# The first layer's input: norm gains applied behind the transposition, quarters of x prepared between the products

## The chip, the cores and the metric

The kernel runs on one core of a Trainium2 chip. The metric is the device time of one execution in microseconds; lower is better. The core has TensorE (PE in the profile, its weight loads PEld), VectorE (DVE), ScalarE (ACT), GpSimd (POOL), the SyncE queue that issues the transfers (SP), and 16 DMA engines.

## The reference

Two transformer-like blocks follow one another on x of 256 tokens by 1024 channels, in float32. What the change touches is the entrance of the first layer of the first block:

```
h = rmsnorm(x, norm1_g[l])          # x * rsqrt(mean(x*x) + eps) * g
z = h @ w_in[l]                     # w_in[l]: 1024 x 6616
z_mla, z_nsa, z_fox, z_dsa, z_gate = split_cols(z, ...)
```

Four mixers work on the columns of z (latent attention, MLA, takes the first 416), gates mix them, w_out and a feed-forward layer follow, all of it twice, and then the second block. The division by the root mean square is by token, the gain g by channel.

## The kernel before

The 256 tokens are two tiles t = 0, 1 of 128. A product needs its left side transposed (channels on the partitions), in chunks k of 128 channels: xT holds 8 chunks for both tiles. Every float32 matrix is split into a rounded part and a rest (h or "hi", and lo), and each product of a chunk is three matmuls: hi by hi (L189), hi by lo (L190), lo by hi (L195). For an xT of 8 chunks and one block of columns, a tile takes 24 matmuls, in two groups of 12 (`products`, L184).

Weights come through `unit` (L60): four chunks by up to 512 columns, as two transfers into `raw` (two chunks each, 504 KB here), then for each half a cast to `whi` on ACT (L85) and a subtraction to `wlo` on DVE (L88). `raw` has six buffers. `steps` (L108) runs, for one block of columns, over k0 = 0 and 4: one unit, then the group of t = 0 and the group of t = 1, so the first block of 504 columns of w_in is four groups of 12 products: (k0 0, t 0), (0, 1), (4, 0), (4, 1). In this text they are steps 1 to 4. `zc(0)` is that block.

x is prepared in quarters (t, c), c a half of the channels. `prep_half` (L392) multiplies a quarter by the gain on DVE (`xg`, L396); `split_T` transposes four chunks on PE into a PSUM tile `tp` (L218), one ACT cast makes xTh (L236) and one DVE subtraction xTl (L237). `square` (L402) takes sums of squares by token on ACT, and `rms_stats` (L407) makes of them on POOL the factor by which the products are scaled when they leave PSUM (L533, L535).

`block1` (L428) writes the order at the start by hand: x(0,0) and the first half of the gain, broadcast to 128 partitions, are loaded; quarter (0,0) is prepared; then the first unit is loaded, with x(0,1) and the second half of the gain between its two transfers; quarter (0,1); then both quarters of t = 1, and the squares. `spin` (L267) puts 12 matmuls on constants ahead of all this on PE.

The framework is a planner: it schedules every engine's instructions in an order of its own, by priority (the order of the program) among what its cost model holds ready, and draws the waits. `issue_after(ins)` keeps what is traced under it behind `ins` on the engine of `ins`, and says nothing to other engines. An engine runs its queue in that order, whatever is late.

After `zc(0)` come `rope_tables` (28 small memsets, a chain of small DVE operations, two sines on ACT, copies on POOL), constants on POOL, and MLA interleaved with the next blocks of columns; MLA normalises its part of z with a POOL power (`rsq`, L257) and transposes the result on PE.

Of the kernel before, what the change touches and what calls it, by code (L numbers as in the profile page):

```python
# [9 lines left out]
F32 = mybir.dt.float32  # L10
# [4 lines left out]
AF = mybir.ActivationFunctionType  # L15
ALU = mybir.AluOpType
AX = mybir.AxisListType

P = 128
T = 256  # L20
D = 1024
# [18 lines left out]
class Net:  # L40
# [16 lines left out]

    def unit(self, w, k0, nk, c0, cn, after=None):  # L60
        nc = self.nc
        if self.ready is not None:
            r, self.ready = self.ready, None
            return r
        src = w.rearrange("(k p) n -> p k n", p=P)
        raws = []
        for i in range(0, nk, 2):
            m = min(2, nk - i)
            raw = self.raw_half()
            nc.sync.dma_start(raw[:, :m, :cn], src[:, k0 + i:k0 + i + m, c0:c0 + cn])  # L70
            raws.append(raw)
            if i == 0 and after is not None:
                after()
        hs, ls = [], []
        for k in range(0, nk, 2):
            for _ in range(min(self.bg_rate // 2, len(self.bg))):
                self.bg.pop(0)()
            m, raw = min(2, nk - k), raws[k // 2]
            self.count += 1
            wp, sfx, nb = self.wp, "", 5  # L80
            if self.wp2 and self.count % 7 in (3, 6):
                wp, sfx, nb = self.wp2, "2", 2
            h = wp.tile([P, 2, 512], F32R, name="whi" + sfx, bufs=nb)
            lo = wp.tile([P, 2, 512], F32R, name="wlo" + sfx, bufs=nb)
            nc.scalar.copy(h[:, :m, :cn], raw[:, :m, :cn])  # L85
            self.turn += 1
            eng = nc.gpsimd if self.share and self.share[self.turn % len(self.share)] else nc.vector
            eng.tensor_sub(lo[:, :m, :cn], raw[:, :m, :cn], h[:, :m, :cn].bitcast(F32))  # L88
# [95 lines left out]
    def products(self, o, xT, k0, t, hs, ls, first, last, within=None):  # L184
        nc, n = self.nc, len(hs)
        later, self.later = self.later, []
        for k in range(n):
            sh, sl = self.chunk(xT, k0 + k, t)
            nc.tensor.matmul(o, sh, hs[k], start=first and k == 0, stop=False)  # L189
            nc.tensor.matmul(o, sh, ls[k], start=False, stop=False)  # L190
            if k == 2 and within is not None:
                within()
            if k % 2 == 1 or k == n - 1:
                for j in range(k - k % 2, k + 1):
                    nc.tensor.matmul(o, self.chunk(xT, k0 + j, t)[1], hs[j], start=False, stop=last and j == n - 1)  # L195
        for f in later:
            f()
# [78 lines left out]

    def constants(self):
        nc, c = self.nc, self.const
        self.spin(12)
        self.ident = c.tile([P, P], F32, name="ident")  # L280
        ones = c.tile([P, 2, P], F32, name="ones")
        nc.vector.memset(ones, 1.0)
# [106 lines left out]

    def prep_half(self, t, c, g, xT, ssq, square=True):  # L392
        nc = self.nc
        sl = slice(c * 512, (c + 1) * 512)
        xg = self.act.tile([P, 512], F32, name="xg", bufs=2)
        nc.vector.tensor_mul(xg, self.x[t][:, sl], g[:, sl])  # L396
        last = self.split_T(xg, 4, xT, c * 4, t)
        if square:
            self.square(t, c, ssq)
        return last  # L400

    def square(self, t, c, ssq):  # L402
        junk = self.act.tile([P, 512], BF16, name="junk", bufs=1)
# [3 lines left out]
    def rms_stats(self, ssq, what):  # L407
# [11 lines left out]
            return r, h  # L419
        return r, None  # L420

    def new_xT(self):
        return self.pair(self.act, 8, "xT")

# [3 lines left out]
    def block1(self):  # L428
        nc, a = self.nc, self.a
        xT, ssq = self.new_xT(), self.new_ssq()  # L430
        x = a["x"]
        g = self.act.tile([P, D], F32, name="gain", bufs=1)
        src = a["norm1_g"][0]

        def load(t, c):
            sl = slice(c * 512, (c + 1) * 512)
            nc.sync.dma_start(self.x[t][:, sl], x[0, t * P:(t + 1) * P, sl])

        def load_gain(c):
            nc.sync.dma_start(g[:, c * 512:(c + 1) * 512],  # L440
                              bass.AP(tensor=src.tensor, offset=src.offset + c * 512, ap=[[0, P], [1, 512]]))

        def second():
            load(0, 1)
            load_gain(1)

        load(0, 0)
        load_gain(0)
        last = self.prep_half(0, 0, g, xT, ssq[0], square=False)
        with self.tc.issue_after(last[0].ins), self.tc.issue_after(last[1].ins):  # L450
            self.ready = self.unit(a["w_in"][0], 0, 4, 0, 504, after=second)
            last = self.prep_half(0, 1, g, xT, ssq[0], square=False)
        with self.tc.issue_after(last[0].ins), self.tc.issue_after(last[1].ins):
            for c in range(2):
                load(1, c)
            for c in range(2):
                self.prep_half(1, c, g, xT, ssq[1])
            for c in range(2):
                self.square(0, c, ssq[0])
        with self.tc.tile_pool(name="b1const", bufs=1) as cpool:  # L460
            self.cpool = cpool
            for l in range(DEPTH):
                r = [self.rms_stats(ssq[t], "half") for t in range(2)]
                xT, ssq = self.attn_layer(l, xT, r)
                r2 = [self.rms_stats(ssq[t], "square")[1] for t in range(2)]
                if l < DEPTH - 1:
                    xT, ssq = self.ff_layer(l, xT, r2)
        self.mp = self.ctx.enter_context(self.tc.tile_pool(name="mem", bufs=1))
        self.block2_constants(self.mp)
        self.memory()  # L470
        return self.ff_layer(DEPTH - 1, xT, r2)[1]
# [48 lines left out]
                self.linear(hT, D_FF // P, a["w_down"][l], [(0, 512), (512, 512)], ev_down)  # L520
        return nxT, ssq

    def attn_layer(self, l, xT, r):
        nc, a = self.nc, self.a
        w = a["w_in"][l]
        with self.tc.tile_pool(name=f"attn{l}", bufs=1) as pool:
# [11 lines left out]
            zc = lambda i: self.steps(xT, 8, w, [(i * 504, 504)], ev_z)  # L538
# [32 lines left out]
            def run(*fill):  # L571
                for f in fill:
                    yield from f

            for _ in zc(0):
                pass
            if l == 0:
                self.rope_tables(self.cpool)
                self.block1_constants(self.cpool)
            self.interleave(self.mla(l, z, oT[0]), run(zc(1), zc(2), zc(3)))  # L580
            self.flush_later()
            self.interleave(self.nsa(l, z, oT[1]), run(zc(4), gates(0), gates(1)))
# [8 lines left out]
            nxT, ssq = self.new_xT(), self.new_ssq()  # L591
# [879 lines left out]
```

## Time and profile before

| | us |
|---|---|
| median of 3 runs | 1733.2 (1732.5 to 1733.45) |
| profiled execution, its own time | 1731.31 |
| its span | 1729.6 |
| PE busy | 1685.1 (97%) |
| DVE busy | 1140.7 (66%) |
| ACT busy | 859.0 (50%) |
| POOL busy | 253.9 (15%) |
| DMA read from HBM | 287.58 MB |

Busy shares are averages over the whole span; the change touches the first 30 us or so of it. The time is the profiled execution's span and 1.7 us around it. PE's clock has two levels, 1.2 and 2.4 GHz; the profile gives the granted share, 0.50 and 1.00.

### The profile page before, as it was taken

To read this page: it belongs to the slowest core of one execution; us is meant where nothing else is said; L and a number is where in the kernel's file an instruction comes from. 1 tells how busy PE (TensorE), PEld (TensorE's weight loads), DVE (VectorE), ACT (ScalarE), POOL (GpSimd) and SP (SyncE) were. 2 spreads that over 40 slices of the span, in tenths; PEclk is the share of its full clock that TensorE was granted. 3 is DMA by queue.
4 is the path that set the end of the run, shared out by engine and by line. 5 is a ranking of instruction groups with operands and counts; after the bars stand their busy time and mean duration, and the time that the engine had idled before them with its cause. 6 is when DMAs were issued, how large, how long until landed. Compare 5 with 4: busy or idle time off the path is not lost. (4 is left out here: it accounts for less than half of the span.)

```text
span 1729.6 us, 22754 instructions
## 1 busy us (share of the span) xinstructions
PE 1685.1 (97%) x8388; PEld 1371.0 (79%) x8388; DVE 1140.7 (66%) x1783; ACT 859.0 (50%) x1300; POOL 253.9 (15%) x283
## 2 busy tenths in 40 slices
PE   8999899999999999999999999999999999999998
PEld 5787678888778767788887977878888977878887
DVE  5766866655466596766456879675555887776554
ACT  5655455554455545555345645444443554544441
POOL 3210100000121011100006830000002850000001
PEclk9999999999999999999999999999999999999999
DMA  7554436555664543665556635366465644456471
GB/s 249 146 146 146 130 120 201 174 183 180 198 167 138 149 124 121 203 196 180 186 181 189 215 127 176 114 196 187 151 220 178 207 145 140 151 191 177 144 226 54
DMA packets 160887, 290.12 MB, mean 168 GB/s; under 512 B 18150, under 2 KB 42056, under 8 KB 160776
## 3 DMA queue, kind: packets, MB, share of 16 engines
q1 hardware_dynamic: 160776, 288.67, 54.5%
q8 instruction: 66, 1.08, 0.3%
q14 instruction: 45, 0.37, 0.1%
HBM read 287.58 MB, written 1.05 MB: 167 GB/s over the span
## 5 line engine op out<-in xcount | busy, mean ns | idle before, releaser
L88 DVE TENSOR_TENSOR wlo<-raw,whi 128x1024 fp32r<-128x1024 f32 (+3 forms) x472 | 571.1, 1214 | 345.1 <-ACT whi L85 338.5
L85 ACT CAST whi<-raw 128x1024 fp32r<-128x1024 f32 (+4 forms) x536 | 546.2, 1022 | 437.3 <-PE mm L195 336.4
L189 PE MATMUL mm<-whi,xTh 128*128 128x512 f32 (+3 forms) x1344 | 522.0, 389 | 3.6 <-DVE th L562 2.1
L190 PE MATMUL mm<-wlo,xTh 128*128 128x512 f32 (+3 forms) x1344 | 512.8, 383 | 0.3 <-DVE wlo L88 0.3
L195 PE MATMUL mm<-whi,xTl 128*128 128x512 f32 (+3 forms) x1344 | 405.4, 382 | 2.2 <-DVE xTl L237 2.0
L189 PEld LDWEIGHTS mm<-whi,xTh 128*128 128x128 f32 x1344 | 253.2, 188 | 49.8 <-DVE th L562 3.0
L195 PEld LDWEIGHTS mm<-whi,xTl 128*128 128x128 f32 x1344 | 249.1, 188 | 51.4 <-DVE xTl L237 4.6
L190 PEld LDWEIGHTS mm<-wlo,xTh 128*128 128x128 f32 x1344 | 253.4, 189 | 42.9 <-DVE wlo L88 1.0
L88 POOL TENSOR_TENSOR wlo<-raw,whi 128x776 fp32r<-128x776 f32 (+1 forms) x64 | 136.7, 2158 | 41.2 <-ACT whi L85 35.9
L257 POOL TENSOR_TENSOR rsq<-rse,mhalf 128x1 f32<-128x1 f32 (+2 forms) x32 | 27.4, 858 | 600.8 <-DVE rse L255 600.8
L189 PE MATMUL mm<-whi,hTh 128*128 128x512 f32 x192 | 76.1, 396 | 0.0
L190 PE MATMUL mm<-wlo,hTh 128*128 128x512 f32 x192 | 75.7, 394 | 0.0
L195 PE MATMUL mm<-whi,hTl 128*128 128x512 f32 x192 | 60.2, 394 | 0.0
L1194 DVE SCALAR_TENSOR_TENSOR mm<-uT,convwT,mm 128x256 f32<-128x256 f32 x120 | 57.8, 481 | 0.1
L1194 DVE SCALAR_TENSOR_TENSOR O<-uT,convwT,O 128x256 f32<-128x256 f32 x120 | 57.8, 481 | 0.0
L189 PE MATMUL mm<-whi,oTh 128*128 128x512 f32 (+1 forms) x140 | 56.6, 404 | 0.0
L190 PE MATMUL mm<-wlo,oTh 128*128 128x512 f32 (+1 forms) x140 | 55.6, 397 | 0.0
L189 PE MATMUL mm<-whi,memTh 128*128 128x512 f32 x128 | 52.7, 412 | 0.0
L190 PE MATMUL mm<-wlo,memTh 128*128 128x512 f32 x128 | 51.0, 399 | 0.0
L410 POOL TENSOR_TENSOR ms<-ssq 128x1 f32<-128x1 f32 x8 | 1.9, 249 | 309.4 <-ACT junk L404 309.3
L236 ACT CAST xTh<-tp 128x512 fp32r<-128x512 f32 x48 | 28.0, 585 | 39.0 <-PE tp L218 37.3
L613 ACT ACTIVATE pexp<-S,nmax 128x128 f32<-128x128 f32 (+1 forms) x80 | 32.6, 419 | 28.6 <-DVE nmax L609 28.4
(404 smaller groups left out, 2367.1 us busy)
## 6 DMA issues: line engine op xcount, KB each, us to landing
raw<-in_w_in SPq DMA_DIRECT2D x80, 512.0 KB, 3.7
raw<-in_w_ffn_in SPq DMA_DIRECT2D x80, 512.0 KB, 4.5
raw<-in_w_up SPq DMA_DIRECT2D x64, 512.0 KB, 3.7
raw<-in_w_down SPq DMA_DIRECT2D x64, 512.0 KB, 4.1
raw<-in_w_ffn_out SPq DMA_DIRECT2D x44, 512.0 KB, 4.2
raw<-in_w_in SPq DMA_DIRECT2D x40, 504.0 KB, 4.2
raw<-in_w_xkv SPq DMA_DIRECT2D x32, 512.0 KB, 4.3
raw<-in_w_in SPq DMA_DIRECT2D x32, 388.0 KB, 3.7
```

The source lines that it names most:

```text
L85: nc.scalar.copy(h[:, :m, :cn], raw[:, :m, :cn])
L88: eng.tensor_sub(lo[:, :m, :cn], raw[:, :m, :cn], h[:, :m, :cn].bitcast(F32))
L189: nc.tensor.matmul(o, sh, hs[k], start=first and k == 0, stop=False)
L190: nc.tensor.matmul(o, sh, ls[k], start=False, stop=False)
L195: nc.tensor.matmul(o, self.chunk(xT, k0 + j, t)[1], hs[j], start=False, stop=last and j == n - 1)
L236: a = nc.scalar.copy(h, tp)
L257: nc.gpsimd.tensor_tensor(r, e, self.mhalf[:, :n], op=ALU.pow)
L410: nc.gpsimd.tensor_tensor(s, ssq[:, 0:1], ssq[:, 1:2], op=ALU.add)
L613: nc.scalar.activation(pe[:, h, :nk], S[h % 2][:, h // 2, :nk], AF.Exp, bias=nm[:, h:h + 1], accum_out=sums[:, h:h + 1])
L1194: nc.vector.scalar_tensor_tensor(o, u, cwT[:, g, j:j + 1], o, op0=ALU.mult, op1=ALU.add)
```

## The change

- The first norm's gain is no longer broadcast over 128 partitions (two transfers of 256 KB). Its row of 1024 is loaded once as 8 by 128 (4 KB), transposed on PE to gT (128 by 8, one column for a chunk), and applied behind the transposition of x: for each chunk an ACT activation with gT as the scale makes the hi part and a DVE operation (times gT, minus hi) the lo part. The DVE multiplication to `xg` goes. For a quarter that is four ACT and four DVE operations of 128x128 instead of one and two of 128x512.
- The spin is 7 matmuls instead of 12. Two matmuls of the identity by quarter (0,0) are added behind that quarter.
- Only quarter (0,0) is prepared ahead of `zc(0)`. Quarters (1,0), (0,1) and (1,1) are loaded and prepared by a hook behind steps 1, 2 and 3. Their ACT and DVE work stands behind that of the quarter before; their PE transposes stand behind the fourth product of the step just traced (`self.second`). The next step is traced behind the new quarter on ACT and DVE, the weights' casts of step 3 among it.
- The squares and `rms_stats` of tile 0 follow quarter (0,1), those of tile 1 quarter (1,1). `rope_tables` and the constants are traced behind the last quarter's ACT and DVE work.
- Later layers keep `prep_half` with a broadcast gain.

```diff
-    def unit(self, w, k0, nk, c0, cn, after=None):
...
+    def unit(self, w, k0, nk, c0, cn):
...
-            if i == 0 and after is not None:
-                after()
...
-            nc.tensor.matmul(o, sh, ls[k], start=False, stop=False)
+            m = nc.tensor.matmul(o, sh, ls[k], start=False, stop=False)
+            if k == 1:
+                self.second = m
...
-        self.spin(12)
+        self.spin(7)
...
+    def order_after(self, ops):
+        s = ExitStack()
+        for o in ops:
+            s.enter_context(self.tc.issue_after(o.ins))
+        return s
...
+        g8 = self.act.tile([P, 512], F32, name="xg", bufs=2)[0:8, :P]
+        gT = self.const.tile([P, 8], F32, name="gainT")
...
-        def second():
-            load(0, 1)
-            load_gain(1)
-
+        def prep(t, c):
+
+            tp = self.transposes([self.x[t][:, c * 512 + k * P:c * 512 + (k + 1) * P] for k in range(4)])
+            for k in range(4):
+                i = c * 4 + k
+                h, lo = self.chunk(xT, i, t)
+                last = (nc.scalar.activation(h, tp[:, k], AF.Copy, scale=gT[:, i:i + 1]),
+                        nc.vector.scalar_tensor_tensor(lo, tp[:, k], gT[:, i:i + 1], h.bitcast(F32),
+                                                       op0=ALU.mult, op1=ALU.subtract))
+            return last
+
+        def arrive(i):
+
+            if i < 3:
+                c, t = (i + 1) // 2, (i + 1) % 2
+                load(t, c)
+                with self.order_after(self.arrived), self.order_after([self.second]):
+                    self.arrived = prep(t, c)
+                if c == 1:
+                    with self.order_after(self.arrived):
+                        for h in range(2):
+                            self.square(t, h, ssq[t])
+                        r.append(self.rms_stats(ssq[t], "half"))
+
+        nc.sync.dma_start(g8, a["norm1_g"][0].rearrange("(k p) -> k p", p=P))
         load(0, 0)
-        load_gain(0)
-        last = self.prep_half(0, 0, g, xT, ssq[0], square=False)
-        with self.tc.issue_after(last[0].ins), self.tc.issue_after(last[1].ins):
-            self.ready = self.unit(a["w_in"][0], 0, 4, 0, 504, after=second)
-            last = self.prep_half(0, 1, g, xT, ssq[0], square=False)
-        with self.tc.issue_after(last[0].ins), self.tc.issue_after(last[1].ins):
-            for c in range(2):
-                load(1, c)
-            for c in range(2):
-                self.prep_half(1, c, g, xT, ssq[1])
-            for c in range(2):
-                self.square(0, c, ssq[0])
+        tg = self.ptp.tile([P, 4, P], F32, name="tp")
+        nc.tensor.transpose(tg[:, 0, :8], g8, self.ident[0:8, 0:8])
+        nc.vector.tensor_copy(gT, tg[:, 0, :8])
+        self.arrived = prep(0, 0)
+        junk = self.pO.tile([P, 4, P], F32, name="O")
+        for _ in range(2):
+            nc.tensor.matmul(junk, self.ident_r, xT[0][:, 0:4, :P], start=True, stop=True)
...
-            for _ in zc(0):
+            first = zc(0)
+            for i in range(4):
+                with self.order_after(self.arrived if hook is not None else ()):
+                    next(first)
+                if hook is not None:
+                    hook(i)
+            for _ in first:
                 pass
             if l == 0:
-                self.rope_tables(self.cpool)
-                self.block1_constants(self.cpool)
+                with self.order_after(self.arrived):
+                    self.rope_tables(self.cpool)
+                    self.block1_constants(self.cpool)
```

## Rows read from the trace of the kernel before

**Rows 1.** Stretches: us, busy (instructions) by engine, granted clock, DMA share, GB/s

```profile
6.60:9.60 3.00, 1.36 (x7) 0.88 (x7) 1.23 (x6) 1.52 (x2) 0.00 (x0) 1.00 0.89 339
9.60:11.70 2.10, 1.11 (x4) 0.72 (x4) 1.81 (x2) 0.56 (x1) 0.00 (x0) 0.51 1.05 408
11.70:16.80 5.10, 4.94 (x12) 3.46 (x11) 2.61 (x4) 3.42 (x6) 0.00 (x0) 0.53 1.07 365
...
18.80:26.80 8.00, 8.00 (x35) 6.31 (x34) 6.77 (x17) 6.65 (x13) 5.27 (x7) 1.00 0.83 259
...
40.00:1729.60 1689.60, 1653.00 (x8266) 1348.89 (x8264) 1116.41 (x1706) 836.71 (x1259) 237.93 (x232) 1.00 0.54 166
```

**Rows 2.** Timeline of DVE to 21 us: start, duration, operation, [idle before and releaser]

```profile
6.02 0.69 DVE L396 TENSOR_TENSOR xg<-x,gain 128x512 f32<-128x512 f32 x1 [3.63 <-DMA gain<-in_norm_g]
...
9.85 0.69 DVE L396 TENSOR_TENSOR xg<-x,gain 128x512 f32<-128x512 f32 x1 [1.01 <-DMA gain<-in_norm_g]
10.46 1.20 DVE L88 TENSOR_TENSOR wlo<-raw,whi 128x1008 fp32r<-128x1008 f32 x1
```

**Rows 3.** Timeline of ACT to 21 us

```profile
8.00 1.03 ACT L85 CAST whi<-raw 128x1008 fp32r<-128x1008 f32 x1
...
16.81 0.63 ACT L404 ACTIVATE junk<-x 128x512 bf16<-128x512 f32 x1
...
17.56 0.63 ACT L404 ACTIVATE junk<-x 128x512 bf16<-128x512 f32 x1
```

**Rows 4.** Timeline of PE, to 17 us and at the end of the first block

```profile
1.53 5.07 PE L275 MATMUL O<-junk 128*128 128x512 bf16 x12 [1.53 <-DVE junk L272]
...
9.09 0.50 PE L189 MATMUL mm<-whi,xTh 128*128 128x504 f32 x1 [1.37 <-ACT whi L85]
10.59 1.12 PE L218 MATMUL tp<-ident,xg 128*128 128x128 f32 x4 [1.00 <-DVE xg L396]
11.71 0.79 PE L190 MATMUL mm<-wlo,xTh 128*128 128x504 f32 x1
...
26.18 0.62 PE L195 MATMUL mm<-whi,xTl 128*128 128x504 f32 x2
```

**Rows 5.** Transfers: SP's issues, landing times (last number, us), DMA rate of two stretches

```profile
0.81 0.39 SPq L437 DMA_DIRECT2D x<-in_x  x1
1.25 0.42 SPq L440 DMA_DIRECT2D gain<-in_norm_g  x1
1.72 0.43 SPq L70 DMA_DIRECT2D raw<-in_w_in  x1
...
x<-in_x SPq DMA_DIRECT2D x1, 256.0 KB, 3.1
...
fox_b<-in_fox_f_bias SPq DMA_DIRECT2D x1, 2.0 KB, 3.1
...
2.80:4.80 2.00, 2.00 (x6) 0.72 (x5) 0.00 (x0) 0.00 (x0) 1.91 (x10) 1.00 0.94 135
5.20:7.20 2.00, 1.73 (x7) 0.67 (x6) 1.12 (x5) 0.00 (x0) 1.04 (x2) 1.00 1.01 380
```

**Rows 6.** Groups of operations by line and shape: busy us, mean ns of one

```profile
L236 ACT CAST oTh<-tp 128x128 fp32r<-128x128 f32 x4 | 1.1, 271 | 0.0
...
L237 DVE TENSOR_TENSOR oTl<-tp,oTh 128x128 fp32r<-128x128 f32 x4 | 1.1, 281 | 0.0
```

**Rows 7.** Timelines of POOL and PE behind the first block, around MLA's normalisation

```profile
31.47 0.88 POOL L374 COPY cos<-cs 128x32 f32<-128x32 f32 x6
...
33.62 0.73 POOL L257 TENSOR_TENSOR rsq<-rse,mhalf 128x2 f32<-128x2 f32 x1
...
35.01 0.56 PE L218 MATMUL tp<-ident,z 128*128 128x128 f32 x3 [2.67 <-DVE z L709]
```

More of the change, by code (lines that the diff above doesn't have):

```diff
@@ L56, in __init__ @@
         self.x = [self.act.tile([P, D], F32, name=f"x{t}") for t in range(2)]
-    def unit(self, w, k0, nk, c0, cn, after=None):
+    def unit(self, w, k0, nk, c0, cn):
         nc = self.nc
-        if self.ready is not None:
-            r, self.ready = self.ready, None
-            return r
         src = w.rearrange("(k p) n -> p k n", p=P)
@@ L388, in apply_rope, with prep_half @@
         eng.tensor_tensor(view[:, :, :rot], view[:, :, :rot], u, op=ALU.add)
-    def prep_half(self, t, c, g, xT, ssq, square=True):
+    def prep_half(self, t, c, g, xT, ssq):
         nc = self.nc
@@ L396, in prep_half @@
         nc.vector.tensor_mul(xg, self.x[t][:, sl], g[:, sl])
[L397 to L400, printed above, removed]
+        self.split_T(xg, 4, xT, c * 4, t)
+        self.square(t, c, ssq)
     def square(self, t, c, ssq):
@@ L430, in block1 @@
         xT, ssq = self.new_xT(), self.new_ssq()
-        x = a["x"]
-        g = self.act.tile([P, D], F32, name="gain", bufs=1)
-        src = a["norm1_g"][0]
+        g8 = self.act.tile([P, 512], F32, name="xg", bufs=2)[0:8, :P]
+        gT = self.const.tile([P, 8], F32, name="gainT")
+        r = []
         def load(t, c):
             sl = slice(c * 512, (c + 1) * 512)
[L437 to L441, printed above, removed]
@@ L443, in second @@
-        def second():
-            load(0, 1)
-            load_gain(1)
-        load(0, 0)
-        load_gain(0)
-        last = self.prep_half(0, 0, g, xT, ssq[0], square=False)
-        with self.tc.issue_after(last[0].ins), self.tc.issue_after(last[1].ins):
-            self.ready = self.unit(a["w_in"][0], 0, 4, 0, 504, after=second)
-            last = self.prep_half(0, 1, g, xT, ssq[0], square=False)
-        with self.tc.issue_after(last[0].ins), self.tc.issue_after(last[1].ins):
-            for c in range(2):
-                load(1, c)
-            for c in range(2):
-                self.prep_half(1, c, g, xT, ssq[1])
-            for c in range(2):
-                self.square(0, c, ssq[0])
+            nc.sync.dma_start(self.x[t][:, sl], a["x"][0, t * P:(t + 1) * P, sl])
@@ L462, in block1 @@
             for l in range(DEPTH):
-                r = [self.rms_stats(ssq[t], "half") for t in range(2)]
-                xT, ssq = self.attn_layer(l, xT, r)
+                if l > 0:
+                    r = [self.rms_stats(ssq[t], "half") for t in range(2)]
+                xT, ssq = self.attn_layer(l, xT, r, arrive if l == 0 else None)
                 r2 = [self.rms_stats(ssq[t], "square")[1] for t in range(2)]
@@ L521, in ff_layer, with attn_layer @@
         return nxT, ssq
-    def attn_layer(self, l, xT, r):
+    def attn_layer(self, l, xT, r, hook=None):
         nc, a = self.nc, self.a
```

## The prediction, made before the changed kernel was run

> **What bounds the kernel now.** I read the busy time by stretches first, then the timelines of PE, DVE and ACT over the first 36 us, then the transfers. From 40 us to the end PE is busy 1653.0 of 1689.6 us at full clock [rows 1]: that part is PE's own work, and whatever PE gains before it should be carried to the end. The change works in the first block of columns, which ends at 26.80 (26.18 and 0.62) [rows 4]. Its 48 products would take 11.0 us at the pace of 18.8 to 26.8, 8.00 us for 35, or 0.229 us each [rows 1]. The reader is to see where the rest goes.
>
> Up to 6.02 DVE waits for a gain, not for x: 3.63 us of idle time end with the transfer of `gain` [rows 2]. While the first broadcast runs, 2.8 to 4.8, the DMA moves 135 GB/s at 94% busy, against 380 GB/s at 5.2 to 7.2 [rows 5]. The second half of the gain does more harm: DVE runs in order, and the multiplication of quarter (0,1) stands ahead of the first wlo. It waits for its gain until 9.85, so wlo runs at 10.46 although its whi was ready at 9.03 (8.00 and 1.03) [rows 2, 3]. PE did its first product at 9.09 and got to the second at 11.71 [rows 4]. In that gap the clock fell: the granted share is 1.00 from 6.6 to 9.6, where PE was busy 1.36 of 3.0 us, and 0.51 to 0.53 from 9.6 to 16.8. There 12 instructions took 4.94 us, 0.41 each [rows 1].
>
> **Term 1, the first products.** The spin's pace is 5.07/12 = 0.42 us, so 7 end at 4.5 instead of 6.6 [rows 4]. x(0,0) takes the second place in SP's queue, issued at about 1.25, and lands 3.1 later as the first transfer did: 4.35 [rows 5]. The gain's 4 KB goes first, at 0.81; no transfer of that kind is in the trace, and the nearest is one of 2 KB that took 3.1: 3.9, hidden under the spin [rows 5]. Five transposes follow, 0.28 us each if at half clock (1.12 for four) [rows 4]: 4.5 to 5.9. The ACT operations of 128x128 take 0.27 each and run behind the transposes one by one [rows 6], so the last ends near 6.2, and whi takes 6.2 to 7.2 [rows 3]; the copy of gT on DVE lies under the transposes, the four DVE operations (0.28 each) under whi. Nothing of a gain stands ahead of wlo now: 7.25 to 8.45, at 1.20 [rows 2]. The second product starts at 8.5 instead of 11.71: **3.2 us earlier**. The two added matmuls wait for the hi part and fit before whi; they cost nothing unless whi were earlier.
>
> Bounds: with transposes at full clock it is 3.9. The other end is the weights. The two transfers ahead of and in raw are 760 KB, 2.0 us at 380 GB/s from the start near 1.6, and the first x shows about 1 us between its last byte and its landing: raw lands near 5. The row says only that it had landed by 8.00, where ACT took it up [rows 3]; if it were still that late, the second product comes at 10.3, and the term is 1.4.
>
> **Term 2, from there to the end of the block.** Before it takes 15.1 us (11.71 to 26.80) [rows 4]. After: 47 products at 0.229, 10.8; three quarters of four transposes at half of 1.12, 1.7; 0.2 for the last matmul to end; and idle time. Step 1 doesn't wait: wlo of the second half is there at 9.65, when PE is still at transposes. Step 2 ends too early for step 3. Its weights' cast stands on ACT behind quarter (0,1), whose transposes stand behind the fourth product of step 2. From the end of these transposes: 0.35 for ACT's last chunks, perhaps a square (0.75, the distance of two squares [rows 3]), whi 1.03, wlo 1.25. That is 3.4 us with a square, 2.6 without; PE has 8 products and the first of step 3 to cover it, 2.1. Idle 0.5 to 1.3; I take 1.3, as the squares are traced earlier than the cast. Quarter (1,1) is covered by the 8 products behind its transposes (1.8, against 0.35 on ACT and 0.3 on DVE). Sum 14.0: **1.1 us shorter**, if the clock stays at 1.00. The gain in DVE work (one 128x512 multiplication of 0.69 for each quarter [rows 2]) is not counted, since DVE isn't last in any of this.
>
> **Term 3, behind the block.** Two squares of tile 1 and four ACT operations for each quarter crowd into the last 4 us, beside the evacuation of tile 0 and the next casts; the 28 memsets and the rope chain now start behind the last quarter. No row shows that order; ACT was busy 6.65 of 8.00 us from 18.8 to 26.8 [rows 1], so 0 to 0.8 is lost: 0.5. SP's loads of positions and of MLA's gains move behind x(1,1), which costs nothing, as they are needed some 10 us later. The wait of 2.67 us at 35.01, where MLA's rsq ran at 33.62, behind six cos copies from 31.47 and what follows them on POOL [rows 7], I leave as long as it is. No added wait stands in SP's queue.
>
> Sum: 3.2 + 1.1 - 0.5 = 3.8 us. The events are those of the profiled execution (1731.31, span 1729.6), which is 1.9 below the median of the runs; taken from the median, 1733.2 - 3.8 = 1729.4.
>
> **The rivals.**
> *The clock falls all the same.* PE's stretch from 6.6 to 9.6 was busy 1.36 of 3.0 us, and the clock fell [rows 1]; after, it holds the added matmuls, one product and 1.1 us from 8.5 on, some 2 us, hardly double. For it: 5 spin matmuls are gone. Against: the idle time of 1.37 us ahead of the first product [rows 4] shrinks to two of under 1 us. If 10 products run at 0.41, 1.8 us go: 1731.3. The Trainium skill ("TensorE: Matmul & The Clock Gate", Part 4: PE-mode transpose) says that transposes don't count as activity for the clock; this speaks against the change, which puts transposes in the place of spin matmuls, and by it this rival would be the likelier one. The trace neither bears it out nor denies it: transposes from 10.59 to 11.71 ran at the low clock, and it rose only when products had run on to 16.8 [rows 1, 4].
> *The weights come no earlier.* Then term 1 is 1.4, the sum 2.0 and the time 1731.2 at full clock. For it: SP's queue held no transfer that landed sooner than 3.1 after its issue, and raw's own landing isn't seen. Against: the 2 us that the gain took are gone from ahead of it [rows 5]. The same time results if 1.8 of the gain go into the wait at 35.01 [rows 7].
> *More than forecast.* With the rms factors done earlier and the rope tables behind MLA's rsq on POOL, the wait of 2.67 goes too [rows 7]: 1726.7.
> *Slower.* The idle time between steps 2 and 3 is the place: if it is as long as that ahead of the second product before (9.6 to 10.6 idle and transposes to 11.7 [rows 4]), as it would be with both squares ahead of the cast, the clock falls a second time. Steps 3 and 4 are 24 products at 0.41, 4.3 us lost, and 10 more in the next block, 1.8; with the first fall (1.8) and term 3 doubled (0.5) the 3.8 become -4.6: 1737.8. [...]
>
> **How the numbers follow.** Forecast 0.43, clock 0.20, weights 0.09, more 0.17, slower 0.11. A measurement of this kernel can tell about 0.2%, 3.5 us, from no change. The forecast's own range is 1728 to 1731 (idle 0.5 to 1.3, term 3 from 0 to 0.8, term 1 to 3.9), and 0.3 of its 0.43 lies over 3.5 us of gain; with the 0.17 and 0.03 of the clock case that is 0.50 for faster. Slower is 0.11, the rest 0.39. The range goes from 1726.2, under the better case, to 1733.4, over the weights' case; it leaves out the slower one and a little of the better.
>
> **What would show it.** Right: the first transposes near 4.6, no wait for a gain on DVE, the second product near 8.5, granted clock 1.00 through 9.6 to 16.8, one idle time of about 1 us ahead of step 3's L190, the block's end near 22.6, and from there the same stretches as before, shifted. Wrong: ACT's first whi waiting for raw; a clock of 0.50 behind 9.6; an idle time of over 2 us ahead of step 3; a longer wait of PE for MLA's z. The forecast is wrong too if the planner, which orders the whole program anew, moves stretches that the change doesn't touch.

## The result and the profile after

The changed kernel takes 1745.78 us (median of 6 runs, 1744.27 to 1747.79) against 1733.33 (6 runs, 1732.38 to 1735.58): a ratio of 1.0069, 95% interval 1.0058 to 1.0079. It is 12 us slower; 1729.4 was forecast, within 1726.2 to 1733.4. The profiled execution took 1746.04, its span is 1744.3. One execution among all the runs below, of e3_delay, took 2779.7 us at a granted clock of 0.555; no ratio counts it.

I compared the two traces by the start of the same PE instruction ("shift": after minus before). It is +4.8 us at 60 us and drifts to +6.5 at 1395 (drifts of up to 3.7 us, most of them upward, stand between the trace of before and the others; it is of an execution 1.9 below its median). Then it goes to +14.6 within 45 us and stays. So there are two losses, one at the start, one late, where the change touched nothing.

**The start.** Stretches of after, columns as in [rows 1]:

```profile
6.60:9.60 3.00, 0.73 (x2) 0.30 (x2) 1.19 (x4) 2.00 (x5) 0.00 (x0) 1.00 1.01 374
9.60:11.70 2.10, 1.34 (x3) 0.87 (x4) 2.04 (x2) 0.96 (x2) 0.00 (x0) 0.58 1.08 358
11.70:16.80 5.10, 5.07 (x15) 3.66 (x13) 0.29 (x1) 0.00 (x0) 0.00 (x0) 0.50 0.89 294
...
18.80:26.80 8.00, 3.20 (x14) 2.09 (x13) 3.45 (x8) 4.87 (x12) 0.59 (x1) 0.80 0.15 56
26.80:40.00 13.20, 13.20 (x51) 10.22 (x52) 8.76 (x44) 9.61 (x24) 2.31 (x6) 0.86 0.65 205
40.00:1744.30 1704.30, 1662.20 (x8287) 1355.50 (x8285) 1130.86 (x1726) 841.69 (x1269) 247.75 (x256) 1.00 0.54 165
```

From 18.8 to 26.8 PE is busy 3.20 us where it was busy all 8.00 before, and the granted clock falls twice: to 0.58 and 0.50 from 9.6 to 16.8, and, after 1.00 in between, to 0.80 and 0.86 from 18.8 to 40. The timeline of PE shows what it waits for (last bracket: idle time before, and what ended it):

```profile
8.76 0.73 PE L472 MATMUL O<-xTh,ident_r 128*128 128x512 f32 x2 [2.39 <-ACT xTh L446]
9.68 0.57 PE L184 MATMUL mm<-whi,xTh 128*128 128x504 f32 x1 [0.19 <-ACT whi L80]
10.93 0.79 PE L185 MATMUL mm<-wlo,xTh 128*128 128x504 f32 x1 [0.68 <-DVE wlo L83]
...
25.35 0.79 PE L184 MATMUL mm<-whi,xTh 128*128 128x504 f32 x1 [4.35 <-ACT whi L80]
26.59 0.79 PE L185 MATMUL mm<-wlo,xTh 128*128 128x504 f32 x1 [0.45 <-DVE wlo L83]
```

The second product comes at 10.93, not at 8.5, and step 3 waits 4.35. ACT and DVE show why, in the first quarter:

```profile
5.98 0.37 ACT L446 ACTIVATE xTh<-tp,gainT 128x128 fp32r<-128x128 f32 x1 [3.53 <-PE tp L215]
6.76 0.37 ACT L446 ACTIVATE xTh<-tp,gainT 128x128 fp32r<-128x128 f32 x1 [0.42 <-DVE xTl L447]
...
8.34 0.37 ACT L446 ACTIVATE xTh<-tp,gainT 128x128 fp32r<-128x128 f32 x1 [0.42 <-DVE xTl L447]
```

```profile
6.38 0.35 DVE L447 SCALAR_TENSOR_TENSOR xTl<-tp,gainT,xTh 128x128 fp32r<-128x128 f32 x1 [1.28 <-ACT xTh L446]
7.17 0.35 DVE L447 SCALAR_TENSOR_TENSOR xTl<-tp,gainT,xTh 128x128 fp32r<-128x128 f32 x1 [0.44 <-ACT xTh L446]
```

The two engines take turns: ACT's second chunk waits for DVE's first, though it needs nothing of its result. One chunk costs 0.78 us, a quarter 3.1 (5.98 to 9.09). The order between them is drawn by the planner: both read the one PSUM tile `tp`. It is so in every quarter. In quarter (0,1) ACT works from 21.04 to 23.77, a square follows, then the cast for step 3 at 24.27. PE has done 48 products, as many as the first block holds, at 34.53, 7.7 later than before [rows 4]. Some of them are already the next block's: step 4 waits for the last chunk of quarter (1,1), and its last product ends at 37.70. Some 3 us of the 7.7 come back, since PE has no more idle time from 26.8 to 40, where before it had the 2.67 of [rows 7]. PE in after, then the stretch in before:

```profile
37.21 0.49 PE L192 MATMUL mm<-whi,xTl 128*128 128x504 f32 x1
```

```profile
26.80:40.00 13.20, 9.96 (x46) 7.92 (x47) 7.92 (x17) 6.58 (x15) 6.08 (x23) 1.00 0.64 195
```

**The late loss.** In the GLA mixer of the second block's second layer (gla_n and gla_z are tiles of it; between its operations DVE works on a convolution), DVE's operations in after:

```profile
1387.41 3.80 DVE L1264 SCALAR_TENSOR_TENSOR gla_n<-gla_z 128x512 f32<-128x512 f32 x1 [0.56 <-ACT gla_z L1261]
...
1402.67 2.26 DVE L1297 TENSOR_TENSOR gla_n<-pj,gla_n 128x256 f32<-128x256 f32 x2
1405.64 2.62 DVE L1349 SCALAR_TENSOR_TENSOR gla_z<-gla_z,pj 128x512 f32<-128x512 f32 x1
1408.57 2.50 DVE L1350 TENSOR_TENSOR gla_z<-gla_z,gla_g 128x512 f32<-128x512 f32 x1
```

In before these took 1.35, 0.74 (two together), 0.68 and 0.68; the first of them:

```profile
1380.92 1.35 DVE L1243 SCALAR_TENSOR_TENSOR gla_n<-gla_z 128x512 f32<-128x512 f32 x1 [0.56 <-ACT gla_z L1240]
```

POOL's timeline in after shows it subtracting weights meanwhile, 2.3 to 2.4 us each, many of them back to back:

```profile
1372.20 18.45 POOL L83 TENSOR_TENSOR wlo<-raw,whi 128x776 fp32r<-128x776 f32 x8 [0.87 <-ACT whi L80]
1394.83 9.48 POOL L83 TENSOR_TENSOR wlo<-raw,whi 128x1024 fp32r<-128x1024 f32 x4 [4.18 <-ACT whi L80]
1405.31 5.22 POOL L83 TENSOR_TENSOR wlo<-raw,whi 128x1024 fp32r<-128x1024 f32 x2 [0.99 <-ACT whi L80]
```

The timeline of PE shows two waits behind it:

```profile
1413.79 0.63 PE L215 MATMUL tp<-ident,xg 128*128 128x128 f32 x4 [1.88 <-DVE gla_en L1295]
1420.65 2.04 PE L1304 MATMUL S<-pj,gla_n 64*128 64x256 f32 x4 [3.36 <-DVE gla_s L1312]
```

Then the granted clock is 0.68 from 1420 to 1430. Idle time and clock together make the 8.1. Every engine's order there is that of before.

The Trainium skill ("SBUF — State Buffer", SBUF: two separate sides) says that a DVE operation with two inputs in SBUF and a GpSimd operation that reads SBUF exclude one another for a whole instruction. The rows agree: POOL reads `raw` and `whi` from SBUF, and these operations of DVE, with both inputs in SBUF, were the long ones, while the convolution's, with one input in PSUM, stayed at 0.48 us between them.

### The profile page after: what moved, and what is told of

It reads as the page before. It is cut to its first block, busy times and chain, and to the rows that moved or that the text cites. A ratio compares the mean times of both kernels' runs of the same rounds, so it can differ in the third digit from the quotient of the medians.

```text
span 1744.3 us, 22763 instructions
## 1 busy us (share of the span) xinstructions
PE 1692.1 (97%) x8386; PEld 1375.9 (79%) x8386; DVE 1149.3 (66%) x1792; ACT 862.2 (49%) x1312; POOL 255.3 (15%) x283
## 5 line engine op out<-in xcount | busy, mean ns | idle before, releaser
L192 PE MATMUL mm<-whi,oTl 128*128 128x512 f32 (+1 forms) x140 | 46.8, 401 | 0.0
```

## The experiments

### Turns on one tile

**e1_two_passes**: the four ACT operations of a quarter traced first, then the four of DVE.

```diff
+            for k in range(4):
+                ha = nc.scalar.activation(hl[k][0], tp[:, k], AF.Copy, scale=gs[k])
             for k in range(4):
...
-                last = (nc.scalar.activation(h, tp[:, k], AF.Copy, scale=gT[:, i:i + 1]),
-                        nc.vector.scalar_tensor_tensor(lo, tp[:, k], gT[:, i:i + 1], h.bitcast(F32),
+                la = nc.vector.scalar_tensor_tensor(hl[k][1], tp[:, k], gs[k], hl[k][0].bitcast(F32),
```

> The changed kernel with one thing different: in each quarter the four ACT operations are traced first and the four DVE operations behind them, instead of in turn. Theory A (two engines are not let at the same PSUM bank at once, so that ACT's next chunk waits for DVE's last one, 0.79 us a chunk): the four ACT operations run on at about 0.26, the four DVE ones behind them at about 0.27, a quarter takes about 2.2 us instead of 3.1; the second product comes near 10.1 instead of 10.93, the wait ahead of step 3 falls from 4.35 to about 3.4, and the first block ends 1.5 to 2 us earlier. Theory B (the operations are slow by themselves, or by the scale read from a column): the distance of two chunks on ACT stays near 0.8 and the time stays. On the loss at 1381 to 1429 us theory C (a matter of the phase of DVE and POOL, not of the start's code) says that it can go or stay here, with 8 us in one step: near 1744 or near 1736.

1730.49 (8 runs), ratio 0.9979 (0.9967 to 0.9991): faster than both kernels, by the order of tracing alone. The turns are gone, and the waits shrink, the one ahead of step 3 to 1.16, where 3.4 was expected (timeline of ACT, then of PE):

```profile
5.98 1.14 ACT L446 ACTIVATE xTh<-tp,gainT 128x128 fp32r<-128x128 f32 x4 [3.53 <-PE tp L215]
```

```profile
9.45 0.79 PE L185 MATMUL mm<-wlo,xTh 128*128 128x504 f32 x1 [0.57 <-DVE wlo L83]
...
19.79 0.50 PE L184 MATMUL mm<-whi,xTh 128*128 128x504 f32 x1 [1.16 <-ACT whi L80]
21.03 0.79 PE L185 MATMUL mm<-wlo,xTh 128*128 128x504 f32 x1 [0.75 <-DVE wlo L83]
```

48 products are done at 28.42, 6.1 earlier than in the changed kernel, and the shift at 60 us is -1.8 instead of +4.8. So the turns are the loss at the start. But 28.42 is still 1.6 later than before; what puts e1 ahead comes behind it, where PE is busy 13.14 of 13.20 us from 26.8 to 40. ACT still begins at 5.98, behind the last of the four transposes (they end at 5.95).

**f2_two_banks**: two `tp` tiles of two chunks for a quarter, two ACT and two DVE operations on each.

```diff
-            tp = self.transposes([... for k in range(4)])
+            for j in (0, 2):
+                tp = self.transposes([... for k in (j, j + 1)])
```

> The changed kernel with each quarter transposed into two PSUM tiles (two banks) of two chunks, for each two ACT operations, then two DVE operations. Theory A (one bank, one engine at a time): ACT goes on to the second tile while DVE works on the first; a quarter takes about 1.7 us from ACT's first to DVE's last operation, against 3.1 as changed and 2.2 with four and four in one bank. Second product near 9.4, wait ahead of step 3 about 1 us, by 60 us of the trace 2 to 3 us ahead of before, time 1729 to 1731. Rival (not the bank, but the order in which the operations were traced): as with four and four, no faster.

1733.39 (10 runs), ratio 0.9998 (0.9989 to 1.0008). ACT starts at 5.55, the second product at 8.91, the earliest of all; the shift at 60 us is -0.5. But PE now reaches step 3 earlier and waits 2.54 there for the same cast (18.80 against e1's 18.69), and the granted clock from 18.8 to 26.8 is 0.57, against 0.79 in e1. What was gained ahead of a wait was given to the wait and to the clock behind it; the 1729 to 1731 expected were missed.

**e2_one_pass**: DVE multiplies the whole tile by gT spread over 128 columns, to SBUF; ACT casts and DVE subtracts from there.

```diff
+            nc.vector.tensor_tensor(u, tp, bc(gT[:, c * 4:c * 4 + 4], 2, P), op=ALU.mult)
+            last = (nc.scalar.copy(h, u), nc.vector.tensor_sub(lo, u, h.bitcast(F32)))
```

> The changed kernel with the gain applied in one pass for a quarter: DVE multiplies the whole transposed tile of 128x512 by gT, each column spread over its chunk, into SBUF; ACT casts it and DVE subtracts, 128x512 each. Loads, order and spin as changed. Theory A: a quarter takes 0.69 + 0.58 + 0.69, about 2.0 us instead of 3.1, and ACT is free 1.1 us after the transposes' end; second product near 9.8, the wait ahead of step 3 about 2.5 us, block's end 2.5 to 3.5 us earlier than in the changed kernel, which is still 1 to 2 us later than before. Rival (the order by quarters is all of the loss): the wait ahead of step 3 stays over 4 us. For the late stretch as for the first run: near 1743 if the loss at 1381 to 1429 stays, near 1735 if it goes.

1735.87, ratio 1.0012 (1.0002 to 1.0023). The second product comes at 9.08, yet PE waits 1.43 for xTh at 16.36 and 2.98 ahead of step 3: each quarter is now a chain of DVE, ACT, DVE, and ACT's cast begins only behind DVE's product. The shift at 60 is +2.2: fewer instructions, but no better than two passes.

### One part of the change at a time

**e4_gain_chunks**: the gain behind the transposition, chunk by chunk, in the order of before, spin of 12.

```diff
-        last = self.prep_half(0, 0, g, xT, ssq[0], square=False)
+        last = prep(0, 0)
```

> Part 1 of the change alone: the gain's row loaded once, transposed, applied chunk by chunk behind the transposition of x; the order of loads, weights and quarters, the squares and the spin of 12 as before. Theory A: the four quarters take 3.1 us each on ACT and DVE in turn; no wait for a gain is left, but the first wlo comes at about 10.3 as before, and the block ends 1 to 3 us later than before: 1734 to 1737, without the late loss. Rival (the loss at the start is from the order by quarters): the block ends 1 to 2 us earlier than before, 1731 to 1732.

1737.38, ratio 1.0021 (1.0012 to 1.0031); the second product at 13.90, behind a wait of 2.45 for wlo. The first quarter took its turns here too (7.26 to 10.37), but they aren't the whole of that wait: whi was ready near 10.9, and DVE had a cast of the positions in its queue ahead of wlo (`pos_f`, at 12.31), which waited 1.94 for their transfer. So e4 loses with the turns in the old order of quarters, but how much of it is theirs it doesn't show.

**e5_weights_free**: the changed kernel, with the weights of steps 3 and 4 not traced behind a quarter.

```diff
-                with self.order_after(self.arrived if hook is not None else ()):
+                with self.order_after(self.arrived if hook is not None and i in (0, 1) else ()):
```

> The changed kernel, but the weights' cast and subtraction of the second unit are no longer held behind quarter (0,1) on ACT and DVE; quarters stay chunk by chunk, ACT and DVE in turn. Theory A (the turns are the main loss): step 3 still needs quarter (0,1), which is 3.1 us long, so the wait ahead of it falls from 4.35 to about 2 us, and 2 of the 4.8 us lost by 60 us of the trace come back. Rival (the order by quarters is the loss): nearly all of the 4.8 comes back. Late loss as in the others: there or not, 8 us.

1739.45, ratio 1.0029 (1.0017 to 1.0041), shift +4.2 at 60 us. The 4.35 ahead of step 3 is gone, but 2.62 for xTh stands at 18.01 and 2.22 for z at 51.11. Holding the weights behind the quarter isn't the loss by itself: something else was late next. The planner gave the first 60 us another order too, so this tells no more than that.

### How much an early start is worth

**e3_delay** and **g3_delay_more**: the kernel before with 32 and 72 spin matmuls instead of 12. **f1_spin8**: the changed kernel with 8 instead of 7.

```diff
-        self.spin(12)
+        self.spin(32)
```

> The kernel before with 32 spin matmuls instead of 12: 8.4 us more on PE at the start and nothing else. The transfers go on under them, so the first block should end some 4 us later, no more. Theory C (the loss of 8 us at 1381 to 1429 comes from the phase at which everything arrives there, and any shift of the start can bring it): this kernel can show it too, then near 1745; DVE's first operation on gla_n of the second layer takes 3.8 us instead of 1.35. Rival (it comes with the changed code): 1737, and that operation takes 1.35.

1733.07, ratio 0.9995 (0.9985 to 1.0005). The first product comes at 11.14 instead of 9.09, the second at 12.65 instead of 11.71. But the products then ran 0.23 apart instead of 0.42, the clock stayed at 1.00, and the block ended 0.6 earlier than before (26.21), not 4 later as expected. Two microseconds of start cost nothing against the clock.

> The kernel before with 72 spin matmuls instead of 12, nothing else. With 32 the first product came 2.05 later, the clock stayed at 1.00 and the time was the same. 40 more at 0.213 us each put it 8.5 later again; with the idle times of 0.46, 0.81 and 0.33 absorbed, PE should be about 6.3 us later at 60 us, as much as the changed kernel is later ahead of the second layer's GLA. Theory (the late loss needs only that shift): gla_n of the second layer takes 3.8 us in some executions and the time goes to 1745 to 1747 there. Rival (a shift alone doesn't bring it): all times near 1739 (ratio 1.0036).

1737.51 (10 runs, none over 1739.7), ratio 1.0024 (1.0015 to 1.0034). Shift +5.1 at 60, +5.2 at 1395 and at 1440; gla_n took 1.35. With the first product 12.7 us later only 5 reach the end of the trace, and 4 the times. And a shift of 5.2 alone doesn't bring the late loss.

> The changed kernel with 8 spin matmuls instead of 7: 0.42 us more at the start, all else unaltered. Theory C (phase): the late loss of about 8 us can vanish by so small an edit; then the time is near 1739, all of the remaining loss lying in the first block. If the late loss belongs to the changed code, 1746.

1745.42 (4 runs), ratio 1.0065 (1.0048 to 1.0081): the late loss is there (gla_n 3.78, shift +6.8 at 1395, +13.8 at 1440). The spin has no part in it.

### The late loss

**f0_again** and **g0_timed**: the changed kernel, unaltered.

> The changed kernel, unaltered, profiled once more, for the stretch at 1381 to 1429 us, where the instructions of all engines stand in the same order as before. If DVE's first operation on gla_n of the second layer loses its place to POOL's next operation by chance alone (theory C, chance), a second profile can show 1.35 us for it and a time near 1738. If the changed kernel always arrives there in the same way, it shows 3.8 us again and a time near 1745.

1737.79, and without the late loss: shift +6.2 at 1395, +6.3 at 1440. The same program, the same operation, in f0's timeline of DVE:

```profile
1387.14 1.39 DVE L1264 SCALAR_TENSOR_TENSOR gla_n<-gla_z 128x512 f32<-128x512 f32 x1 [0.56 <-ACT gla_z L1261]
```

POOL's operation beside it ended 0.84 after gla_n's start in f0, 0.86 in after. In f0 DVE went next and POOL waited; in after POOL's next went first.

> The changed kernel, unaltered, timed once more. In one profile of it the DVE operation gla_n of the second layer took 3.80 us, waiting out a POOL operation, and the end came 14.6 us late; in another it took 1.39 and the end came 6.3 late. Theory (which of the two engines gets in at the boundary of POOL's operations is settled anew in each execution): times lie in two groups, near 1738 and near 1745, with nothing between. Rival (it belongs to the chip or to the runs of that hour): all times lie in one group, either near 1738 or near 1745. The part lost at the start is in all of them: no time under 1736.

1744.47 to 1746.2 (4 runs), gla_n 3.82, with a shift of 5.3 ahead of it. So 1738 is the exception, one of 11 runs, and the group forecast by the rival is the rule. g3, with the same shift of 5.2, never had it: it is not how late PE is, but how DVE and POOL stand to each other. In the traces with the loss POOL's next operation began 0.803 to 0.817 us after gla_n's start, in those without 0.737 to 0.805 (all in the second layer; in the first, after itself had 0.803 and no loss). A matter of tens of nanoseconds, and the two overlap: what decides it stays open. Nor is it the chip: f1, with the loss, ran on the one on which f0 ran without.

**g1_psum_operand**: gla_n and the first gla_z take an operand from the PSUM bank instead of SBUF.

```diff
-            nc.vector.scalar_tensor_tensor(n, zs, -1.0, zs, op0=ALU.mult, op1=ALU.min)
+            nc.vector.scalar_tensor_tensor(n, zp, -1.0, zs, op0=ALU.mult, op1=ALU.min)
```

> The changed kernel, but GLA's two DVE operations gla_n and gla_z take the first operand from the PSUM bank it was copied from, not from SBUF. The convolution's DVE operations, with one operand in PSUM, ran beside the POOL operations at 0.48 us each without a wait. Theory (the late loss is DVE waiting for POOL, because both operands of these operations are in SBUF): gla_n takes under 1 us, the second layer loses nothing, and all times are near 1738 (ratio 1.0025, the start's 4.5 us). Rival (the late loss has another cause, and gla_n only shows it): times near 1745 come as often as with the unaltered kernel (ratio 1.006 to 1.007 if in all).

1747.8, ratio 1.0082 (1.0067 to 1.0097). The operation itself fell to 0.69, beside a running POOL: with one input in PSUM it doesn't wait. But a later one, gla_z (L1350), now took 2.85 and 2.78, in both layers, and 4.4 and 5.7 us were lost there. The planner had also changed DVE's order around, so the next was tried.

**h1_pool_halves**: each POOL subtraction written as two of half the size, every engine's order as in after. **h3_squares_halves**: the same on g2_squares_first (below).

```diff
-            eng.tensor_sub(lo[:, :m, :cn], raw[:, :m, :cn], h[:, :m, :cn].bitcast(F32))
+            step = 1 if eng is nc.gpsimd else m
+            for i in range(0, m, step):
+                eng.tensor_sub(lo[:, i:i + step, :cn], raw[:, i:i + step, :cn], ...)
```

> The changed kernel, but each wlo subtraction on POOL is written as two of half the size, one for each chunk; every engine's order is otherwise that of the changed kernel. In the late loss DVE's gla_n (3.80 us), a second gla_n (1.93) and two gla_z (2.62, 2.50) each waited for a POOL operation of 2.4 us. Theory (DVE waits out whole POOL operations): POOL operations of 1.2 to 1.3 us halve these waits, so gla_n takes at most 2.6 and the late loss goes from 8 to 0 to 4: 1738 to 1742 (ratio 1.0025 to 1.005), no time near 1746. Rival (the waits are a sign of something else that comes 8 us late by itself, such as the transfers of the weights): 1745 to 1747, as before the halving.

1751.94, ratio 1.0104 (1.0087 to 1.0121). The cause was right and the direction wrong (timeline of DVE in both layers, then of POOL in the second):

```profile
983.67 4.72 DVE L1266 SCALAR_TENSOR_TENSOR gla_n<-gla_z 128x512 f32<-128x512 f32 x1 [0.15 <-ACT gla_z L1263]
...
1394.41 4.74 DVE L1266 SCALAR_TENSOR_TENSOR gla_n<-gla_z 128x512 f32<-128x512 f32 x1 [0.47 <-ACT gla_z L1263]
```

```profile
1379.02 19.58 POOL L85 TENSOR_TENSOR wlo<-raw,whi 128x388 fp32r<-128x388 f32 x16 [0.30 <-ACT whi L80]
```

DVE lost at three ends of POOL operations in a row (0.40, 1.65 and 2.92 after its start); it got in at the fourth (4.19), when POOL had nothing ready any more. Now both layers lose, 7.0 and 6.6.

> g2_squares_first with the same halving. g2 had no late loss (gla_n 1.37) in its profile. Theory: nothing is lost there, so there is next to nothing to gain: 1728 to 1730 (ratio 0.997 to 0.998). Rival (POOL's operations cost DVE time in all the stretches where both work, so that halves give some of it back; or twice the instructions on POOL cost more): under 1727, or over 1731.

1743.63, ratio 1.0060 (1.0044 to 1.0077): in a kernel that had no late loss the halves bring it into both layers, 6.7 and 5.4, with gla_n at 4.73 and 4.75. That is the strongest evidence for the mechanism: making POOL hold DVE off for longer makes the loss, where next to nothing was expected to change.

**i1_abs_on_act**: ACT takes |z|, the sign goes into the exponential's scale; gla_n leaves DVE. **i2_filled_abs**: the same on h4_filled (below).

```diff
-            nc.vector.scalar_tensor_tensor(n, zs, -1.0, zs, op0=ALU.mult, op1=ALU.min)
-        nc.scalar.activation(n, n, AF.Exp)
+        nc.scalar.activation(n, zs, AF.Abs)
+        nc.scalar.activation(n, n, AF.Exp, scale=-1.0)
```

> The changed kernel, but -|z| of GLA is no longer made by DVE's gla_n operation: ACT takes the absolute value and puts the sign into the scale of the exponential that follows. PE's, POOL's and SP's orders stay; DVE's lacks the one operation, and some ten neighbours change places. Theory (the late loss begins with that one DVE operation, which POOL keeps out of SBUF, so that ACT's Exp and all behind it come 2.4 to 3.4 us late): near 1738 in all executions (ratio 1.002 to 1.0035), PE at the same shift of 4 to 6 us at 60, 1395 and 1440 us. Rival (any DVE operation of GLA that finds POOL busy will do, such as the later gla_n and gla_z): 1742 to 1746 still.

1746.65, ratio 1.0076 (1.0060 to 1.0093): the rival was right. Without the wait, ACT's casts come earlier, POOL's next pair starts at 1410.16, and gla_z stands just behind it (timeline of DVE, then of POOL):

```profile
1410.32 2.79 DVE L1349 TENSOR_TENSOR gla_z<-gla_z,gla_g 128x512 f32<-128x512 f32 x1
```

```profile
1410.16 5.21 POOL L83 TENSOR_TENSOR wlo<-raw,whi 128x1024 fp32r<-128x1024 f32 x2 [3.41 <-ACT whi L80]
```

3.9 us are lost in each layer. Not one operation is to blame but any of this chain that meets POOL.

> h4_filled with the same edit. h4's profile showed no late loss; gla_n took 1.4 there, waiting for the end of one POOL operation. Theory: the 0.7 us that gla_n waits in each layer isn't on PE's path, since PE had no wait there, so the time is h4's, 1728 to 1730.5 (ratio 0.997 to 0.9985). Rival (it is on the path): 1 to 1.5 us less, under 1728.

1736.79, ratio 1.0021 (1.0012 to 1.0031), with 3.9 lost in each layer where h4 lost nothing. Neither forecast said that: removing a wait of 0.7 from DVE cost 7.5 us (0.43%, 1.0021 against h4's 0.9978).

| kernel | DVE beyond its usual time, second layer's GLA, us | shift gained there, us |
|---|---|---|
| before, f0, g3, e1 to e5, f2, g2, h4 | 0 | 0 to 0.1 |
| i1, i2 | 2.1 (one operation) | 3.9 |
| g1 | 2.1 (one operation) | 5.7 |
| after, g0, f1 | 2.4 + 1.5 + 1.9 + 1.8 | 8.1, 7.8, 7.0 |
| h1 | 3.3 + 1.5 + 0.3 + 0.7 | 6.6 |
| h3 | 3.4 + 1.5 + 0.3 + 0.7 | 5.4 |

(The second column is each duration less 1.39, 0.75 and 0.68, as in f0.)

### What the forecast had meant

**g2_squares_first**: e1 with a tile's squares traced ahead of its second quarter. In e1 the cast for step 3 stood behind a square.

```diff
+                if c == 1:
+                    with self.order_after(self.arrived):
+                        for h in range(2):
+                            self.square(t, h, ssq[t])
                 with self.order_after(self.arrived), self.order_after([self.second]):
                     self.arrived = prep(t, c)
```

> e1_two_passes with the squares of a tile traced ahead of its second quarter instead of behind it: ACT has 1.16 to 5.8 us of idle time there. In e1 the cast for step 3 started at 18.69, behind a square of 0.6, and PE waited 1.16 for it, with the clock falling behind it. Theory (the square is what keeps step 3's weights): that cast starts near 18.1, the wait is 0.5 to 0.7, and the time is 0.5 to 2 us under e1's, 1729 (ratio 0.997); the more if the clock holds at 1.00. Rival (a square that waits for x(0,1) holds ACT, or the planner fills the place with something else): no gain over e1, 1730 to 1732.

1728.91 (8 runs), ratio 0.9977 (0.9966 to 0.9987). The wait ahead of step 3 is 0.65, 48 products are done at 25.82, the shift is -4.3 at 60 and -4.1 at the end. Behind them PE has no wait left:

```profile
26.80:40.00 13.20, 13.15 (x61) 10.50 (x60) 11.51 (x38) 9.04 (x18) 9.33 (x20) 1.00 0.59 167
```

e1 and g2 can't be told apart by their intervals, but both beat before and after.

**h4_filled**: g2 with three matmuls on constants behind the first quarter's transposes, and one more on its hi part.

```diff
+        with self.order_after([self.tr]):
+            for _ in range(3):
+                nc.tensor.matmul(junk, one[:, :P], one, start=True, stop=True)
```

> g2_squares_first with three more matmuls on constants behind the transposes of the first quarter and one more behind its hi part, where PE had 0.99, 0.18 and 0.85 us of idle time between 5.9 and 9.3. In g2 the first 12 products from 9.26 ran 0.42 apart, half of the later pace of 0.23; with 32 spin matmuls the products ran at 0.23 from the first on. Theory (the idle times among the transposes are what kept the clock low there): the products run at 0.23 from the second on, 12 times 0.19 are 2.3 us, and 1 to 2.5 of it arrive at the end: 1726.5 to 1728 (ratio 0.9955 to 0.997). Rival (the next wait takes it: the second quarter's x or step 3's weights aren't there sooner): the waits ahead of step 3 grow by as much, 1728 to 1730.

1729.26 (9 runs), ratio 0.9978 (0.9968 to 0.9987). The theory on the clock holds: stretches of g2, then of h4.

```profile
6.60:9.60 3.00, 1.58 (x4) 0.83 (x5) 2.64 (x6) 2.18 (x4) 0.00 (x0) 0.87 1.00 372
9.60:11.70 2.10, 2.10 (x6) 1.65 (x6) 0.72 (x1) 0.00 (x0) 0.00 (x0) 0.50 1.07 367
```

```profile
6.60:9.60 3.00, 2.15 (x9) 1.42 (x8) 2.44 (x6) 2.38 (x5) 0.00 (x0) 1.00 1.01 380
9.60:11.70 2.10, 2.10 (x10) 1.75 (x11) 0.92 (x1) 0.00 (x0) 0.00 (x0) 1.00 1.05 349
```

Its products ran 0.23 apart from the third on, and the shift at 60 us was -5.4, 1.1 better than g2's. The forecast had 12 products of g2 at 0.42; only those up to the eighth were, so 1.3 us and not 2.3 were to be had. The waits ahead of step 3 didn't grow (0.62 and 0.92), against the rival. In the profiled execution 3.7 of the shift went by the end, in drifts between 100 and 1000 us; i2, with the same start, kept 5.2 of 5.7 to 1000. In the times the gain isn't seen, and the 1726.5 to 1728 expected were missed.

## Why the prediction was wrong, step by step

- **No gain awaited, first transposes near 4.6**: right. DVE copied gT at 4.93, the transposes started at 4.83, raw was no bound.
- **Term 1 (3.2)**: the failed step is "run behind the transposes one by one", so that "the last ends near 6.2". It ended at 8.7. The forecast took ACT's and DVE's chunks as independent, with [rows 6] for their length, and never asked what separates two engines that read one tile. The trace of before had shown it: the grouped rows of the operations that read a `tp` on ACT give DVE's previous reading as a releaser (2.6 us at L239, 4.7 at L660, the row below). The Trainium skill ("PSUM — Partial Sum Buffer", PSUM bank collisions raise a hardware error) says that the compiler's scheduler puts a dependency between any two engines' instructions on one bank and quadrant of 32 partitions, reads included. The trace agrees for this planner: 0.78 us for a chunk in turns, and in e1 0.26 (four of 0.37 in 1.14). It spoke against this change and I hadn't weighed it. The term measured 0.8 (11.71 to 10.93); in e1 it was 2.3, in f2 2.8.

```profile
L660 ACT ACTIVATE qkT<-tp 64x256 fp32r<-64x256 f32 x24 | 9.1, 378 | 8.5 <-DVE qkT L661 4.7 <-PE tp L218 3.7
```

- **Clock at 1.00**: wrong, the rival "the clock falls all the same" came true as a part (0.58 and 0.50). The Trainium skill ("TensorE: Matmul & The Clock Gate", Part 4: PE-mode transpose) was cited for transposes not counting as activity for the clock. g2 and h4 fit it: with h4's three matmuls among the transposes the products stood 0.23 apart from the third on, in g2 0.42 up to the eighth. But those matmuls also filled idle time, and no run here tells the two apart. (The rival's 1731.3 should read 1731.2, the forecast and 1.8.)
- **Term 2 (1.1)**: the step "0.35 for ACT's last chunks" was 2.73. The idle time ahead of step 3 was 4.35 and 0.45, not 1.3, and the clock fell a second time: the mechanism of the rival "slower", at its place, from another cause. From the second product to the 48th it took 23.6 us, where 14.0 was forecast and before took 15.1: 8.5 lost instead of 1.1 gained, the largest part of the loss at the start. f0, with the start's loss alone, took 1737.79; the rival's price was 1737.8, but it was made up of other parts, so that agreement is luck.
- **"The wait of 2.67 I leave as long as it is"**: wrong, in the better direction. PE was busy through 26.8 to 40, and g2 and h4 had no such wait either. This is the rival "more than forecast", and its reason is seen in g2: MLA's two rsq ran on POOL at 29.12 and 31.90, ahead of the sines and cosines (from 34.23), where before the second stood at 33.62 behind six cos copies [rows 7]. With it term 3, 0.5 lost by the forecast, was 2.9 gained in after (7.7 later at the 48th product, 4.8 at 60 us).
- **"Whatever PE gains before it should be carried to the end"**: held for the start's loss to within 2 us, and failed at 1387. No rival had a place there: the planner moved nothing, yet 8.1 us were lost. f0 and after show one program with and without this part: by their times 10 of 11 runs of it had the loss, and none of g3's. Why this program meets it so often stays open.
- **The sum**: a gain of this size was to be had, but not by the forecast's way. g2 gives 4.0 (0.23% of 1733; by its interval 2.3 to 5.9), with waits of 0.65 and 0.92 in step 3. In its trace the second product comes 2.5 earlier (9.26), the stretch from there to the 48th takes 16.6, 1.5 more than before and not 1.1 less, and 3.3 come from behind it. So the forecast's 3.8 agrees with it by luck: term 2 was too good even without the turns, and the wait of 2.67 made up for it.

## What to carry to other kernels

Before splitting an operation into chunks for two engines, look at what they share: on one PSUM tile the order in which chunks are traced becomes an order in time, so trace one engine's whole pass first. Count the quarter's whole length into whatever stands behind it in an engine's queue, and find the next thing that is late, as f2 and e5 show. A chain of DVE operations with both inputs in SBUF beside a busy POOL is a risk to every change ahead of it. No run here shows a cure: an input in PSUM freed the one operation that had it (g1), taking it off DVE freed it too (i1), and both times a later operation of the chain met POOL. An input in PSUM for the whole chain, or no work for POOL there, was not tried.

## What the runs showed of the hardware that I had not expected

- A DVE operation with both inputs in SBUF waited for POOL until POOL had nothing ready, 4.7 us with operations of 1.3; smaller operations on POOL didn't let it in sooner. With one operand in PSUM the same operation took 0.69. Which of the two goes first when an operation of 2.4 ends differed between executions of one program.
- A first product 2.05 us later cost nothing (e3): PE had been busy 3.00 of 3.00 us from 6.6 to 9.6 (1.36 before), and the granted clock then stayed at 1.00 where before it was 0.51 and 0.53.
- In e1 the granted clock reads 1.00 from 9.6 to 11.7, yet its products stood 0.42 apart, nearly twice the later 0.23. Where the two differ, the spacing of equal matmuls is what PE paid.
